# HGRN scores of a unit's two heads in one run of narrow matmuls, far and near parts in one PSUM bank

## The chip, the cores and the metric

The kernel runs on one core of a Trainium2 chip. A core has five engines with their own instruction queues, each of which works in order: TensorE (PE in the profile; its weight loads are listed apart as PEld), VectorE (DVE), ScalarE (ACT), GpSimd (POOL) and SyncE (SP), which issues most of the DMAs. Matmuls write to PSUM, an accumulator memory in banks; the other operands lie in SBUF. The metric is the device time of one execution in microseconds (us), the median of three.

## The reference

One layer of a hybrid decoder trunk on 256 tokens of width 2048. One input projection feeds three mixers of width 1024 (HGRN2, RG-LRU, Mamba-2 SSD) and their gates; each branch goes through its block of the output projection, is gated and added to the residual stream, and a final RMSNorm closes it.

```python
h = rmsnorm(x, norm_w[l])
proj = h @ w_in[l]
o_a = hgrn2_mixer(a_q, a_f, a_i, lower_bounds[l])
o_a = rmsnorm(o_a, hgrn_norm_w[l].reshape(A_HEADS, A_VAL)).reshape(bsz, s, BRANCH_WIDTH)
o_a = o_a * jax.nn.silu(a_z)
...
branch_out = jnp.einsum('bsnc,ncd->bsnd', branches, w_out[l].reshape(N_BRANCH, BRANCH_WIDTH, D_MODEL))
x = x + jnp.sum(gates * branch_out, axis=2).astype(x.dtype)
```

The change lies in `hgrn2_mixer`. It has 8 heads of 128 keys and 128 values. In each head the score of query t against key s is a sum over the keys of q·k times the product of the forget gates between s and t, and the output is the causal scores times the values.

## The kernel before, in words

**The weight stream.** All of the weights (140 tiles of 1 MB, `raw`) are read once by DMA. Each tile is cut into two halves. For each half ScalarE rounds it to `whi` (line 415) and VectorE forms the rest `wlo` (line 417); there are four buffers of each. TensorE uses a half in 12 matmuls of 512 columns (blocks by token: lines 523 to 525, three products for each of four pieces) or in 16 matmuls of 512 and 256 columns in turn (blocks by channel: lines 472 and 473). `whi` of a half can be written only when TensorE is through with the half four before it. These are called weight matmuls below.

**The mixers.** Everything else is written as Python generators ("streams"). A planner with a model clock for each engine (`Clock`, `Engine.cost`, `Streams.fits`) decides at build time between which weight matmuls a piece of a stream is put into the engines' queues. A stream gives way at each `yield`, whose letters name the engines that the next piece needs. The planner's cost of a matmul is four cycles per column, at least as many as for 128 rows or for the rows it loads; it does not know that narrow matmuls can run beside each other. Since the engines work in order, what the planner lays down is the order of execution.

**The HGRN stream.** `a_unit(i)` works on two heads, and there are four units, with their matmuls at about 469, 546, 613 and 689 us. For each head it makes 52 narrow matmuls, each with 32 rows of output, called a score run below: 4 of 128 columns (`px`, scores between the two halves of the sequence), 4 of 64 (`far64`), 4 of 32 (`far32`), and the near scores `pd`: 8 of 48 columns and 32 of 16. Then ScalarE copies `px` into the score tile `sc`, VectorE picks the near scores together in `dg` (one multiply with `id32`, five predicated copies) and copies `far64`, `far32` and `dg` into `sc`: together called the clearing of a head. Then two matmuls multiply `sc` with the values (`vt`): the value matmuls. `sc` has a tile for each of the two heads (`sc_3581` and `sc_3582` in the built program).

When both heads are done, ScalarE squares the output (`osq`), splits it into `two` (the upper part by ScalarE, the rest by VectorE), two matmuls sum the squares over a head (lines 1194 and 1195 before; called the norm matmuls), ScalarE makes the inverse root (three operations, `rq` last), VectorE applies it with the gate, and `split_branch` writes the result as `boh` (ScalarE) and `bol` (VectorE). These are the weights' partner in the output projection of branch 0. Its first block follows right behind the fourth unit: its first three halves of weights meet heads 0 to 5, the fourth half meets heads 6 and 7, which are the fourth unit's.

Before the change, the loop over the two heads holds everything from the score run to the value matmuls; each head takes two PSUM tiles, `pf` (far) and `pd` (near).

## Time and profile before

| | us |
|---|---|
| median of three runs | 830.51 (829.95 to 830.66) |
| the profiled execution | 830.41 |
| its span, from the first to the last instruction | 828.6 |
| PE busy in the span | 815.4 |
| DVE busy | 615.0 |
| ACT busy | 478.3 |

1.8 us of the execution lie outside the span. The span has some 10 us before the stream of weight matmuls starts and some 15 us behind the last one; between them PE is nearly always busy. In a timeline a row has the start in us, the time it covers, the engine, the line, the operation, output and inputs, the sizes and how many instructions of the kind are merged in it (x8), and, in brackets, how long the engine was idle before and what ended that. Line 161 is that of the helper through which all of the streams' operations go, so they are told apart by their tiles. A matmul of full 32-bit numbers, as in the score runs, is recorded twice.

### The profile page before, as it was taken

The numbers are of one execution on the slowest core, as the hardware profiler recorded it, in microseconds if no ns is written. First come the engines' busy times: TensorE is split into PE (matmuls) and PEld (weight loads), VectorE is DVE, ScalarE is ACT, GpSimd is POOL, SyncE is SP. The second block draws the span as 40 slices with busy tenths as digits, with TensorE's granted clock in tenths as the row PEclk, the third lists the DMA queues.
The fourth block names the chain that finished last, engine by engine and source line by source line (L and its number), as shares of the span: only waits on it lengthen the run. The fifth ranks groups of instructions, "written<-read, shape, count | busy, mean of one in ns | idle before, by whom it ended". The sixth has DMA issues, their size and how long they took to land.

```text
span 828.6 us, 12296 instructions
## 1 busy us (share of the span) xinstructions
PE 815.4 (98%) x4805; PEld 683.7 (83%) x4805; DVE 615.0 (74%) x976; ACT 478.3 (58%) x653; POOL 48.4 (6%) x103
## 2 busy tenths in 40 slices
PE   8999999999999999999999999999999999999995
PEld 8978887887888888888888888888888888888884
DVE  6578796987878787668786887688778868656463
ACT  6556455655665747645666556647655673754443
POOL 0000200020120000200100200000020000000000
PEclk9999999999999999999999999999999999999998
DMA  9947745565595555754465645553584455565522
GB/s 338 358 157 252 259 173 189 197 197 197 189 338 198 181 200 183 246 207 161 162 240 203 206 157 198 203 196 117 200 248 157 159 204 198 187 220 202 203 102 102
DMA packets 27401, 167.45 MB, mean 202 GB/s; under 512 B 3808, under 2 KB 4352, under 8 KB 9296
## 3 DMA queue, kind: packets, MB, share of 16 engines
q1 hardware_dynamic: 23360, 153.63, 52.7%
q0 software_dynamic: 3840, 12.96, 5.1%
q8 instruction: 37, 0.61, 0.3%
q10 hardware_dynamic: 144, 0.09, 0.1%
q14 instruction: 20, 0.16, 0.1%
HBM read 161.41 MB, written 5.26 MB: 201 GB/s over the span
## 4 chain that ended last, share of the span: by engine, by line
PE 95%; DVE 2%; ACT 1%; DMA 1%; issue 1%; SPq 0%; POOL 0%; POOLq 0%; DVEq 0%; ACTq 0%
PE ps L523 22%; PE ps L524 22%; PE ps L525 22%; PE ps L472 14%; PE ps L473 7%; PE pmt L161 3%; PE ps L485 2%; DMA raw<-w 1%; PE pmt L962 1%; ACT whi L415 0%; DVE wlo L417 0%; DVE sc L161 0%; ACT l L161 0%; PE ps L543 0%; PE ps L541 0%
## 5 line engine op out<-in xcount | busy, mean ns | idle before, releaser
L417 DVE TENSOR_TENSOR wlo<-raw,whi 128x1024 fp32r<-128x1024 f32 x275 | 332.7, 1221 | 165.7 <-ACT whi L415 165.0
L415 ACT CAST whi<-raw 128x1024 fp32r<-128x1024 f32 x275 | 286.8, 1051 | 286.8 <-PE ps L525 165.4
L523 PE MATMUL ps<-whi,hT 128*128 128x512 f32 x640 | 251.4, 393 | 0.0
L524 PE MATMUL ps<-wlo,hT 128*128 128x512 f32 x640 | 249.3, 390 | 0.0
L525 PE MATMUL ps<-whi,hT 128*128 128x512 f32 x640 | 249.3, 390 | 0.0
L472 PE MATMUL ps<-hT,whi 128*128 128x512 f32 x512 | 181.4, 397 | 0.0
L473 PE MATMUL ps<-hT,wlo 128*128 128x256 f32 x512 | 143.6, 280 | 0.0
L523 PEld LDWEIGHTS ps<-whi,hT 128*128 128x128 f32 x640 | 120.2, 188 | 25.7 <-issue 1.1
L525 PEld LDWEIGHTS ps<-whi,hT 128*128 128x128 f32 x640 | 120.1, 188 | 25.4
L524 PEld LDWEIGHTS ps<-wlo,hT 128*128 128x128 f32 x640 | 120.2, 188 | 24.0
L472 PEld LDWEIGHTS ps<-hT,whi 128*128 128x128 f32 x512 | 96.0, 188 | 23.1 <-issue 0.7
L473 PEld LDWEIGHTS ps<-hT,wlo 128*128 128x128 f32 x512 | 96.7, 189 | 0.5
L523 PE MATMUL ps<-whi,boh 128*128 128x512 f32 x176 | 69.2, 393 | 0.0
L524 PE MATMUL ps<-wlo,boh 128*128 128x512 f32 x176 | 68.6, 390 | 0.0
L525 PE MATMUL ps<-whi,bol 128*128 128x512 f32 x176 | 68.5, 389 | 0.0
L525 PEld LDWEIGHTS ps<-whi,bol 128*128 128x128 f32 x176 | 33.0, 188 | 6.9
L523 PEld LDWEIGHTS ps<-whi,boh 128*128 128x128 f32 x176 | 33.0, 188 | 6.7
L524 PEld LDWEIGHTS ps<-wlo,boh 128*128 128x128 f32 x176 | 33.1, 188 | 6.6
L134 ACT ACT_TABLE_LOAD x26 | 33.4, 1283 | 1.5 <-PEq L1474 1.2
L161 ACT ACTIVATE gt<-ps,rtok 128x512 f32<-128x512 f32 x36 | 23.7, 681 | 7.7 <-PE ps L525 6.9
L693 POOL DMA_DIRECT2D zd<-gt x12 | 6.6, 550 | 359.8 <-DVE gt L161 316.6
L707 POOL DMA_DIRECT2D gz<-zd x48 | 26.2, 552 | 15.0 <-DMA zd<-gt 14.4
(241 smaller groups left out, 669.4 us busy)
## 6 DMA issues: line engine op xcount, KB each, us to landing
raw<-w SPq DMA_DIRECT2D x137, 1024.0 KB, 4.8
zd<-gt POOLq DMA_DIRECT2D x12, 256.0 KB, 2.5
gz<-zd POOLq DMA_DIRECT2D x48, 64.0 KB, 5.1
raw<-w SPq DMA_DIRECT2D x5, 512.0 KB, 8.8
xsq<-xtok SPq DMA_DIRECT2D x2, 1024.0 KB, 10.6
brd<-sums POOLq DMA_DIRECT2D x4, 512.0 KB, 5.6
xacc<-xtok POOLq DMA_DIRECT2D x1, 2048.0 KB, 13.1
out_dram<-xacc SPq DMA_DIRECT2D x7, 256.0 KB, 2.4
```

Source lines behind the costliest of these rows:

```text
L134: self.eng.preload_act_table_set(self.set)
L161: return f(*a, **k)
L415: nc.scalar.copy(out=hi, in_=raw[:, sl])
L417: nc.vector.tensor_tensor(out=lo, in0=raw[:, sl], in1=hi.bitcast(F32), op=ALU.subtract)
L472: pe.matmul(ps[:, ct], lhsT=hi[:, c0:c0 + 128], rhs=flat(hT[:, k]), start=k == 0, stop=False)
L473: pe.matmul(ps[:, ct, S:], lhsT=lo[:, c0:c0 + 128], rhs=hT[:, k, 0], start=False, stop=k == KD - 1)
L485: pe.matmul(ps[:, ct], lhsT=(hi, lo)[i][:, c0:c0 + 128], rhs=hT[:, q * 4 + kk, j], start=q == 0 and n == 0, stop=q == 3 and n == last)
L523: pe.matmul(pss[j], lhsT=hi_ap(k, j), rhs=hi[:, sl], start=k == 0, stop=False)
L524: pe.matmul(pss[j], lhsT=hi_ap(k, j), rhs=lo[:, sl], start=False, stop=False)
L525: pe.matmul(pss[j], lhsT=lo_ap(k, j), rhs=hi[:, sl], start=False, stop=k == nk - 1)
L707: gp.dma_start(out=t[32 * q:32 * q + 32, 4 * j:4 * j + 4], in_=zd[q, :, j])
L962: pe.matmul(o, lhsT=wp[:, a, ct, g], rhs=xp[:, b, ct], start=u == 0, stop=u == 2)
```

## The change

The loop over the two heads is cut into three. The first makes both heads' score runs, one behind the other with no `yield` between them. Each head now has one PSUM tile: `pd` is a view of columns 224 to 447 of `pf`, behind `px`, `far64` and `far32`. The second loop clears the heads, with a `yield` between them. The third does the value matmuls of both.

```diff
         yield from st.get("pm", "p")
         op = pm.tile([P, 2, S], F32, name="pmt")
+        made = []
         for ct in range(2):
-            h = 2 * i + ct
             pf = pm.tile([P, 512], F32, name="pmt")
-            pd = pm.tile([P, 2, 112], F32, name="pmt")
+            pd = pf[:, 224:448].rearrange("p (j n) -> p j n", j=2)
             px, far64, far32 = pf[:, 0:128], pf[:, 128:192], pf[:, 192:224]
...
-            yield "va"
+            made.append((px, far64, far32, pd))
+        yield "va"
+        for ct, (px, far64, far32, pd) in enumerate(made):
             sc = A["sc"][ct]
             scd = sc[:, 0:3:2]
             dg = a2.tile([P, 2, 32], F32, name="dg")
...
             for u in range(0, P, 32):
                 dve.tensor_copy(out=scd[u:u + 32, :, u:u + 32], in_=dg[u:u + 32])
-            yield "p"
+            if ct == 0:
+                yield "va"
+        yield "p"
+        for ct in range(2):
+            h, sc = 2 * i + ct, A["sc"][ct]
             hv = slice(h * P, h * P + P)
             mm.matmul(op[:, ct], lhsT=vt[:, 0, hv], rhs=flat(sc[:, 0:2]), start=True, stop=False)
             mm.matmul(op[:, ct, P:S], lhsT=vt[:, 1, hv], rhs=sc[:, 2], start=False, stop=True)
```

No arithmetic is added or taken away. What moves is the order on each engine, since the planner now places other pieces. Up to the first unit's score runs (469 us) nothing moves. In all four units PE has 104 narrow matmuls in one run where it had 52 twice. Between that run and the first head's value matmuls stand 36 weight matmuls in the first and the fourth unit, 56 by channel in the second, and 15 by token and 28 by channel in the third; the second head's value matmuls follow 3 (by channel: 4) weight matmuls later. The third and fourth unit's runs come 30 weight matmuls later than before. Three places:

The first is on PE behind the fourth unit (`sc_3582` is the second head's score tile, `two` the input of the norm matmuls, `boh` and `bol` the output projection's). Before, the second head's value matmuls stand 24 weight matmuls ahead of the norm matmuls, whose surroundings are:

```order
L523 MATMUL ps<-whi,hT 128x512
L524 MATMUL ps<-wlo,hT 128x512
L525 MATMUL ps<-whi,hT 128x512
L1194 MATMUL pmt<-two,onesr 128x512
L1195 MATMUL pmt<-two,onesr 128x512
L523 MATMUL ps<-whi,hT 128x512
L524 MATMUL ps<-wlo,hT 128x512
L525 MATMUL ps<-whi,hT 128x512
L523 MATMUL ps<-whi,boh 128x512
```

With the change:

```order
L161 MATMUL pmt<-sc_3582,vt 128x256
L161 MATMUL pmt<-sc_3582,vt 128x128
L523 MATMUL ps<-whi,hT 128x512
L524 MATMUL ps<-wlo,hT 128x512
L525 MATMUL ps<-whi,hT 128x512
L1200 MATMUL pmt<-two,onesr 128x512
L1201 MATMUL pmt<-two,onesr 128x512
L523 MATMUL ps<-whi,boh 128x512
```

The norm matmuls stay where they were in the stream of weights, but for three matmuls; the value matmuls moved towards them, so that 3 weight matmuls are left between the two where there were 24.

The second is on ACT at the same place, from the squares of the fourth unit to its `boh` (`gt` is the gate of the output projection's first block):

```order
 L161 ACTIVATE osq<-pmt 128x512
 L161 CAST two<-osq 128x512
-L415 CAST whi<-raw 128x1024 x2
+L161 ACTIVATE gt<-ps,rtok 128x512 x2
 L134 ACT_TABLE_LOAD
 L161 ACTIVATE osq<-pmt,eps 128x512
 L161 ACTIVATE osq<-osq 128x512
 L161 ACTIVATE rq<-osq 128x512
-L134 ACT_TABLE_LOAD
-L161 ACTIVATE gt<-ps,rtok 128x512 x2
 L161 CAST boh<-osq 128x512
```

The two gate operations and the one table load that is left now stand ahead of the inverse root, and two roundings of weights went ahead of the squares or behind `boh`; the next `whi` after `boh` is that of the fourth half of the output projection's first block.

The third is on DVE, where a head is cleared, with the waits in brackets (`dg` collects the near scores; `Activation` is ScalarE's counter). It reads the same in all eight heads:

```order
 L161 TENSOR_TENSOR dg<-pmt,cs 128x64 [waits PE_49]
-L161 COPY_PREDICATED dg<-mk,pmt 128x32 [waits DVE_49]
+L161 COPY_PREDICATED dg<-mk,pmt 128x32 [waits Activation_49]
 L161 COPY_PREDICATED dg<-mk,pmt 128x2x16 [waits DVE_49]
 L161 COPY_PREDICATED dg<-mk,pmt 128x4x8 [waits DVE_49]
 L161 COPY_PREDICATED dg<-mk,pmt 128x8x4 [waits DVE_49]
 L161 COPY_PREDICATED dg<-mk,pmt 128x16x2 [waits DVE_49]
-L161 COPY sc_3581<-pmt 64x64 [waits Activation_49]
+L161 COPY sc_3581<-pmt 64x64 [waits Pool_49]
```

Before, ScalarE's copy of `px` waited for PE alone, and VectorE waited for it where it starts on `far64`. Now the copy waits for VectorE's first operation on the bank, and VectorE's second waits for the copy.

## The prediction

> **What bounds the kernel now.** I read the shares of the engines and the chain of waits first, then the waits between engines by tile, then the timelines of PE, DVE and ACT around the four units. The page's busy line, and from its fourth part the chain by engine:

> ```profile
> span 828.6 us, 12296 instructions
> PE 815.4 (98%) x4805; PEld 683.7 (83%) x4805; DVE 615.0 (74%) x976; ACT 478.3 (58%) x653; POOL 48.4 (6%) x103
> PE 95%; DVE 2%; ACT 1%; DMA 1%; issue 1%; SPq 0%; POOL 0%; POOLq 0%; DVEq 0%; ACTq 0%
> ```

> PE is busy for 815.4 of 828.6 us and makes 95% of the chain that sets the end. So time is won or lost only where PE's own work gets shorter or longer, or where PE stands still. It does stand still in this part of the kernel, but little. The list of waits, for PE on the scores (idle us, times, longest):

> ```profile
> PE pmt L161 <- DVE sc L161: 0.9, 2, 0.7
> ```

> The narrow matmuls, by their tile (count, then least, median and longest ns of one). They are told by pitch, not by these durations, since narrow matmuls lie over one another: 179 ns each times 104 would be 19 us a head.

> ```profile
> L161 PE MATMUL pmt<-ql,kl x640: 179/183/219, 469.6 to 698.3; 128*32 128x16 f32 x128, 128*32 128x64 f32 x16, 128*32 128x32 f32 x16
> ```

> **One run instead of two.** PE in the first unit: the last weight matmuls ahead, the start of the score run, its last group, and two weight matmuls behind.

> ```profile
> 468.84 0.39 PE L524 MATMUL ps<-wlo,hT 128*128 128x512 f32 x1
> 469.07 0.39 PE L525 MATMUL ps<-whi,hT 128*128 128x512 f32 x1
> 469.39 0.43 PE L161 MATMUL pmt<-ql,kx 128*32 128x128 f32 x8
> ...
> 470.27 0.45 PE L161 MATMUL pmt<-ql,kl 128*32 128x16 f32 x31
> 470.65 0.50 PE L523 MATMUL ps<-whi,hT 128*128 128x512 f32 x1
> 470.99 0.40 PE L524 MATMUL ps<-wlo,hT 128*128 128x512 f32 x1
> ```

> Starts are what counts. Two weight matmuls lie 0.23 us apart (468.84 and 469.07). The narrow run starts 0.32 behind the last of them, 0.09 more. At its end the last narrow matmul starts at 470.27 + 0.45 − 0.18 (one lasts 0.18) = 470.54, and the next weight matmul at 470.65: some 0.10 more than the step inside the run. The weight matmul after that comes 0.34 later and not 0.23: another 0.11. So a changeover into narrow matmuls and out of them takes 0.09 + 0.10 + 0.11 = 0.30. The run itself is 470.54 − 469.39 = 1.15 a head. The change makes no matmul fewer; it takes away one changeover in each of four units: 4 × 0.30 = **−1.20**. Not shown before is a second head that follows straight behind the first. If its eight 128-column matmuls bring back part of the 0.09 the saving is 0.20 a unit; if a run's slow start (0.88 for the 128, 64 and 48 columns and first 16, 469.39 to 470.27) is partly filling up, it is 0.45. That makes 0.8 to 1.8; I take 1.20, since it is read from the edges themselves.

> **Waits on the scores that go.** PE in the second unit, at the value matmuls of the first and of the second head, and in the third unit at the second head's:

> ```profile
> 553.11 0.28 PE L473 MATMUL ps<-hT,wlo 128*128 128x256 f32 x1
> 553.22 0.81 PE L161 MATMUL pmt<-sc,vt 128*128 128x256 f32 x4
> 553.79 0.47 PE L472 MATMUL ps<-hT,whi 128*128 128x512 f32 x1
> ...
> 563.68 0.28 PE L473 MATMUL ps<-hT,wlo 128*128 128x256 f32 x1
> 564.70 0.89 PE L161 MATMUL pmt<-sc,vt 128*128 128x256 f32 x4 [0.74 <-DVE sc L161]
> 565.34 0.48 PE L472 MATMUL ps<-hT,whi 128*128 128x512 f32 x1
> ```
> ```profile
> 625.26 0.39 PE L525 MATMUL ps<-whi,bol 128*128 128x512 f32 x1
> 625.82 0.89 PE L161 MATMUL pmt<-sc,vt 128*128 128x256 f32 x4 [0.18 <-DVE sc L161]
> 626.47 0.48 PE L523 MATMUL ps<-whi,boh 128*128 128x512 f32 x1
> ```

> The first head's do not wait: 0.11 from the 256-column matmul ahead, 0.57 to the next. The second head's wait: 1.02 and 0.64, so 0.91 + 0.07 = 0.98 more. In the third unit 0.56 for 0.23 and 0.65 for 0.57: 0.33 + 0.08 = 0.41. Together **−1.39**, if they don't come back. Whether they do is decided by the clearing, on DVE and on ACT in the first unit:

> ```profile
> 470.77 0.22 DVE L161 TENSOR_TENSOR dg<-pmt,cs 128x64 f32<-128x64 f32 x1 [1.01 <-PE pmt L161]
> 471.03 1.18 DVE L161 COPY_PREDICATED dg<-mk,pmt 128x32 f32<-128x32 uint8 x5
> ...
> 474.07 1.23 DVE L417 TENSOR_TENSOR wlo<-raw,whi 128x1024 fp32r<-128x1024 f32 x1
> ```
> ```profile
> 470.11 0.27 ACT L161 COPY sc<-pmt 128x128 f32<-128x128 f32 x1 [1.60 <-PE pmt L161]
> ```

> A head's clearing is 470.77 to 474.07 = 3.30 on DVE. The bank that far and near parts now share adds a handover: DVE's second operation waits for ACT's copy, 0.26 (470.11's 0.27, less what overlaps), and two passes between engines of some 0.04 each: 0.34, so 3.64 a head. From the run's start, the first head is made at 1.15 + 0.18 = 1.33, cleared at 4.97; with one `wlo` (1.23) between, the second at 9.84. PE reaches its value matmuls in units 1 and 4 behind a run of 2.40, 36 weight matmuls of 0.23, the first head's 0.57 and three more weight matmuls with their changeover 0.77: 12.0. In unit 2, 56 matmuls by channel (0.23 and 0.11 in turn: 9.5) put it at 13.3; in unit 3, 15 and 28 of the two kinds (8.2) at 12.0. Were DVE in a `wlo` when the run ends, it is 11.1 instead of 9.84. So 1 to 2 us are left everywhere. The handover is hidden by that cover; if it is gone, all of it stands on PE (third rival). Bounds of this term: 1.39 down to 0.

> What the rows speak against is a price for the shared bank: in before ACT's copy at 470.11 ran while PE was still filling the other bank. [...]

> **The fourth unit's tail.** This is where a new wait comes in. PE in before around the second head's value matmuls, and much later the last weight matmul of the first three halves:

> ```profile
> 702.46 0.39 PE L525 MATMUL ps<-whi,hT 128*128 128x512 f32 x1
> 702.68 0.81 PE L161 MATMUL pmt<-sc,vt 128*128 128x256 f32 x4
> 703.25 0.47 PE L523 MATMUL ps<-whi,hT 128*128 128x512 f32 x1
> ...
> 704.02 0.40 PE L523 MATMUL ps<-whi,hT 128*128 128x512 f32 x1
> ...
> 713.79 0.39 PE L525 MATMUL ps<-whi,bol 128*128 128x512 f32 x1
> ```

> ACT there, from the squares to `boh`:

> ```profile
> 703.53 0.60 ACT L161 ACTIVATE osq<-pmt 128x512 f32<-128x512 f32 x1 [1.65 <-PE pmt L161]
> 704.16 0.62 ACT L161 CAST two<-osq 128x512 fp32r<-128x512 f32 x1
> ...
> 706.96 1.05 ACT L415 CAST whi<-raw 128x1024 fp32r<-128x1024 f32 x1 [1.23 <-PE ps L525]
> ...
> 709.51 0.69 ACT L161 ACTIVATE osq<-pmt,eps 128x512 f32<-128x512 f32 x1 [0.20 <-PE pmt L1195]
> ...
> 711.55 1.28 ACT L134 ACT_TABLE_LOAD   x1
> 712.84 1.27 ACT L161 ACTIVATE gt<-ps,rtok 128x512 f32<-128x512 f32 x2
> ...
> 714.47 0.62 ACT L161 CAST boh<-osq 128x512 fp32r<-128x512 f32 x1 [0.35 <-DVE osq L161]
> 714.99 2.95 ACT L415 CAST whi<-raw 128x1024 fp32r<-128x1024 f32 x3
> ```

> And DVE:

> ```profile
> 706.91 0.69 DVE L161 TENSOR_TENSOR two<-osq,two 128x512 fp32r<-128x512 f32 x1
> ...
> 711.56 0.69 DVE L161 SCALAR_TENSOR_TENSOR rq<-pmt,rq 128x512 f32<-128x512 f32 x1 [2.29 <-ACT rq L161]
> ...
> 713.74 0.69 DVE L161 TENSOR_TENSOR osq<-osq,gz 128x512 f32<-128x512 f32 x1
> ```

> Let X be the start of the second head's value matmuls (702.68 here). ACT's square starts at X + 0.85, its `two` runs from X + 1.48 to 2.10, DVE's `two` takes 0.69 more: X + 2.83. Before, 24 weight matmuls (5.5 us) covered that. Now three are left, so PE is at the norm matmuls at X + 1.34 (704.02 − 702.68), and would leave them at X + 1.79. The first can go at X + 2.12, the second at X + 2.87, the next weight matmul at X + 3.10: PE stands for **1.31**. Queued behind them on PE is the whole of the output projection's first block.

> What is late next is its fourth half. The chain from X: `gt` on ACT 2.10 + 1.27 = 3.37; table load 1.28, 4.65; the three operations of the inverse root 709.51 to 711.53, 2.02, 6.67; DVE from `rq` to the end of `osq`, 711.56 to 714.43, with the handoffs 2.90, 9.57; `boh` 0.04 later until `whi` begins, 714.47 to 714.99, so 10.13; `whi` 1.05, 11.18; its `wlo` 1.23 and 0.04, 12.45. A PE that had waited for nothing would need that `wlo` at the half's second matmul, 36 + 1 behind the norm matmuls: 704.02 to 713.79 are 43 matmuls in 9.77, 0.227 each, so 1.79 + 8.40 = 10.19. PE is late by 12.45 − 10.19 = **+2.26** in all, 1.31 of it at the norm matmuls and 0.95 at the fourth half. Bounds: 1.9 if the half's first matmuls go ahead and two handoffs overlap, 2.7 if DVE has a `wlo` in the way at `two` for part of its 1.23. I take 2.26, since every term has its row.

> **The sum:** −1.20 − 1.39 + 2.26 = −0.33, on the profiled execution's own 830.41 (1.81 of it outside the span): 830.08. The median of the runs shown, 830.51, is 0.10 above that execution, so 830.2. With the bounds: 829.2 (1.8, 1.39 and 1.9 give −1.3) to 831.0 (0.8, half of 1.39 and 2.1 give about +0.5).

> **The rivals.** A difference of 0.2%, 1.66 us (828.85 and 832.17), is about what a measurement of this kernel can tell from no change.

> First, the tail doesn't hold PE: the two savings alone, −2.59, 827.9. For it: the profile's other places show PE covering such chains without a wait (before, the norm matmuls start at their pitch), and a PE that comes to X late finds ACT and DVE free. Against it: nothing in the order lets the norm matmuls go before both `two`, and the wait of 1.31 is counted from X itself. Chance 0.16.

> Second, the joined run saves nothing, since the second head's start and the slow part of the run cost as much inside as at an edge: +1.20 on the forecast, 831.4. For it: 0.88 of a head's 1.15 lie ahead of its last 31 narrow matmuls, so wide and narrow ones aren't alike. Against it: the 0.30 is read at the weight matmuls, which are simply fewer neighbours of narrow ones. Chance 0.12.

> Third, slower: the shared bank's handover stands on PE's path, ahead of the value matmuls. Its price is 8 heads × 0.34 = 2.72, so 832.9, and more with the old waits back. It decides from the point where the second head is cleared more than those 1 to 2 us later than worked out, as when ACT's copy sits behind a `whi` of 1.05 and a second `wlo` of 1.23 slips in. For it: before, PE waited at exactly these matmuls (0.74 and 0.18). Against it: 36 weight matmuls cover now. Chance 0.14.

> **How the numbers follow.** The forecast has 0.58, of which 0.04 lie below 828.85. Faster: 0.16 + 0.04 = 0.20; same: 0.54 + 0.12 = 0.66; slower: 0.14. The range goes from 827.6, which takes in most of the first rival, to 832.0, which takes in the second; the third and the rest of the first are left out, about 0.19.

> **What would show it.** In the changed kernel's PE timeline: one stretch of 2.3 to 2.5 us of narrow matmuls in each unit, with one changeover; no idle time by DVE's `sc` ahead of value matmuls in units 2 and 3; ahead of the norm matmuls (lines 1200 and 1201) idle time of about 1.3 us by `two`, and about 1 us by `whi` or `wlo` some 36 weight matmuls later. On DVE, `dg`'s second operation waits some 0.3 for ACT's `sc`. It is wrong if PE goes through the norm matmuls without a stop, if the fourth half waits much more than 1 us, if waits by `sc` appear anywhere, or if a second head's score run begins with a gap.

## The result and the profile after

The changed kernel takes 838.09 us (median of six, 835.25 to 841.02) and the kernel before, on the same chip, 830.59: a ratio of 1.0091 (95% interval 1.008 to 1.0101), 0.9% slower and clear of the noise. 830.2 was forecast, with 832.0 as the range's upper end. The spread of 5.8 us is new too: before it is 0.7.

The page of the changed kernel, its span, engines and chain:

```profile
span 836.2 us, 12297 instructions
PE 816.5 (98%) x4805; PEld 685.1 (82%) x4805; DVE 614.6 (73%) x976; ACT 478.2 (57%) x653; POOL 48.5 (6%) x103
PE 94%; issue 1%; ACT 1%; DMA 1%; DVE 1%; SPq 0%; POOL 0%; POOLq 0%; DVEq 0%; ACTq 0%
```

The span is 7.6 us longer with the same number of matmuls and nearly the same busy time. "issue" is time in which the engine waited for nothing that the profile shows. The list of waits says whose (total, times, longest):

```profile
PE pmt L161 <- issue: 4.7, 2, 3.8
PE ps L472 <- issue: 1.5, 1, 1.5
```

Neither row is there before, and the waits of PE on DVE's `sc` are gone. PE's timeline shows where it stands: in the joined runs of unit 1 and unit 3, and just behind the run of unit 2.

```profile
470.97 0.26 PE L161 MATMUL pmt<-ql,kl 128*32 128x16 f32 x9
472.12 0.34 PE L161 MATMUL pmt<-ql,kl 128*32 128x16 f32 x19 [0.89 <-issue]
...
472.41 0.46 PE L161 MATMUL pmt<-ql,kl 128*32 128x16 f32 x31
472.80 0.50 PE L523 MATMUL ps<-whi,hT 128*128 128x512 f32 x1
473.14 0.40 PE L524 MATMUL ps<-wlo,hT 128*128 128x512 f32 x1
...
549.62 0.28 PE L473 MATMUL ps<-hT,wlo 128*128 128x256 f32 x1
551.35 0.40 PE L472 MATMUL ps<-hT,whi 128*128 128x512 f32 x1 [1.46 <-issue]
...
622.63 0.21 PE L161 MATMUL pmt<-ql,kl 128*32 128x16 f32 x3
626.63 0.43 PE L161 MATMUL pmt<-ql,kl 128*32 128x16 f32 x28 [3.79 <-issue]
...
627.80 0.53 PE L523 MATMUL ps<-whi,boh 128*128 128x512 f32 x1
628.12 0.63 PE L524 MATMUL ps<-wlo,boh 128*128 128x512 f32 x1
...
631.45 0.39 PE L523 MATMUL ps<-whi,boh 128*128 128x512 f32 x1
```

In units 1 and 3 the matmuls on either side of the gap are of the same kind, in the middle of the second head's near scores: nothing that they read comes from DVE or ACT at that moment. In starts, PE loses 1.05 us in unit 1 (from 471.05, where the last of the nine starts, to 472.12, less a step), 1.62 in unit 2 (1.73 − 0.11) and 3.96 in unit 3. Behind unit 3 the weight matmuls also become slow. By windows (busy time of the engines, then PE's granted clock):

```profile
624.51:627.92 3.41, 1.29 (x32) 1.12 (x32) 0.99 (x6) 0.00 (x0) 0.00 (x0) 1.00 0.21 79
627.92:631.33 3.41, 3.41 (x10) 2.65 (x9) 1.83 (x4) 1.31 (x2) 0.00 (x0) 0.50 0.00 0
```

For 3.41 us the clock is 0.50, and a weight matmul takes 0.43 us and not 0.23: 3.65 us from 627.80 to 631.45 for 9 steps that take 2.05 at full speed, 1.60 lost. Together 1.05 + 1.62 + 3.96 + 1.60 = 8.2 us, which is more than the whole difference. So the rest of the change gained a little, about as forecast, and an unforeseen cost went on top.

The tail of unit 4 in the changed kernel, for later use:

```profile
713.28 0.81 PE L161 MATMUL pmt<-sc,vt 128*128 128x256 f32 x4
...
715.43 0.49 PE L1200 MATMUL pmt<-two,onesr 128*128 128x512 f32 x1 [0.63 <-ACT two L161]
716.16 0.50 PE L1201 MATMUL pmt<-two,onesr 128*128 128x512 f32 x1 [0.23 <-DVE two L161]
716.50 0.40 PE L523 MATMUL ps<-whi,boh 128*128 128x512 f32 x1
...
724.68 0.39 PE L523 MATMUL ps<-whi,boh 128*128 128x512 f32 x1
725.70 0.50 PE L524 MATMUL ps<-wlo,boh 128*128 128x512 f32 x1 [0.64 <-DVE wlo L417]
```

### The profile page after: what moved, and what is told of

Read it like the earlier page. It is cut to its first block, busy times and chain, and to the rows that moved or that the text cites. A ratio compares the mean times of both kernels' runs of the same rounds, so it can differ in the third digit from the quotient of the medians.

```text
span 836.2 us, 12297 instructions
## 1 busy us (share of the span) xinstructions
PE 816.5 (98%) x4805; PEld 685.1 (82%) x4805; DVE 614.6 (73%) x976; ACT 478.2 (57%) x653; POOL 48.5 (6%) x103
## 4 chain that ended last, share of the span: by engine, by line
PE 94%; issue 1%; ACT 1%; DMA 1%; DVE 1%; SPq 0%; POOL 0%; POOLq 0%; DVEq 0%; ACTq 0%
PE ps L523 22%; PE ps L524 22%; PE ps L525 22%; PE ps L472 14%; PE ps L473 7%; PE pmt L161 3%; PE ps L485 2%; DMA xc_t<-xT 1%; PE pmt L962 1%; ACT whi L415 0%; ACT osq L161 0%; PE ps L543 0%; PE ps L542 0%; PE ps L541 0%; DVE xacc L161 0%
## 5 line engine op out<-in xcount | busy, mean ns | idle before, releaser
L417 DVE TENSOR_TENSOR wlo<-raw,whi 128x1024 fp32r<-128x1024 f32 x275 | 332.9, 1220 | 167.1 <-ACT whi L415 166.7
L415 ACT CAST whi<-raw 128x1024 fp32r<-128x1024 f32 x275 | 286.8, 1050 | 281.9 <-PE ps L525 161.0
L523 PE MATMUL ps<-whi,hT 128*128 128x512 f32 x640 | 251.3, 393 | 0.0
L525 PE MATMUL ps<-whi,hT 128*128 128x512 f32 x640 | 249.3, 389 | 0.0
L524 PE MATMUL ps<-wlo,hT 128*128 128x512 f32 x640 | 249.3, 389 | 0.0
L472 PE MATMUL ps<-hT,whi 128*128 128x512 f32 x512 | 181.6, 398 | 1.5 <-issue 1.5
L473 PE MATMUL ps<-hT,wlo 128*128 128x256 f32 x512 | 143.5, 280 | 0.0
L523 PEld LDWEIGHTS ps<-whi,hT 128*128 128x128 f32 x640 | 120.2, 188 | 25.5 <-issue 1.1
L525 PEld LDWEIGHTS ps<-whi,hT 128*128 128x128 f32 x640 | 120.1, 188 | 25.4
L524 PEld LDWEIGHTS ps<-wlo,hT 128*128 128x128 f32 x640 | 120.2, 188 | 24.0
L472 PEld LDWEIGHTS ps<-hT,whi 128*128 128x128 f32 x512 | 96.1, 188 | 23.1 <-issue 0.7
L473 PEld LDWEIGHTS ps<-hT,wlo 128*128 128x128 f32 x512 | 96.7, 189 | 2.0 <-issue 1.5
L524 PE MATMUL ps<-wlo,boh 128*128 128x512 f32 x176 | 69.4, 394 | 0.6 <-DVE wlo L417 0.6
L523 PE MATMUL ps<-whi,boh 128*128 128x512 f32 x176 | 69.4, 394 | 0.0
L525 PE MATMUL ps<-whi,bol 128*128 128x512 f32 x176 | 69.1, 393 | 0.0
L524 PEld LDWEIGHTS ps<-wlo,boh 128*128 128x128 f32 x176 | 33.3, 189 | 7.8 <-DVE wlo L417 1.1
L525 PEld LDWEIGHTS ps<-whi,bol 128*128 128x128 f32 x176 | 33.5, 190 | 7.1
L523 PEld LDWEIGHTS ps<-whi,boh 128*128 128x128 f32 x176 | 33.5, 190 | 6.9
L161 ACT ACTIVATE gt<-ps,rtok 128x512 f32<-128x512 f32 x36 | 23.9, 683 | 7.7 <-PE ps L525 6.9
## 6 DMA issues: line engine op xcount, KB each, us to landing
xsq<-xtok SPq DMA_DIRECT2D x2, 1024.0 KB, 11.1
```

The costliest lines, as they stand in the source:

```text
L161: return f(*a, **k)
L415: nc.scalar.copy(out=hi, in_=raw[:, sl])
L417: nc.vector.tensor_tensor(out=lo, in0=raw[:, sl], in1=hi.bitcast(F32), op=ALU.subtract)
L472: pe.matmul(ps[:, ct], lhsT=hi[:, c0:c0 + 128], rhs=flat(hT[:, k]), start=k == 0, stop=False)
L473: pe.matmul(ps[:, ct, S:], lhsT=lo[:, c0:c0 + 128], rhs=hT[:, k, 0], start=False, stop=k == KD - 1)
L523: pe.matmul(pss[j], lhsT=hi_ap(k, j), rhs=hi[:, sl], start=k == 0, stop=False)
```

## The theories

If PE waits for none of its operands, it may wait for its own instructions. The page has a queue that carries them (packets, MB, share; the same row before and after), the third queue of its third part:

```profile
q8 instruction: 37, 0.61, 0.3%
```

PE runs 4805 weight loads and 4805 matmuls. 0.61 MB over 37 packets is 16.4 KB a packet, and 37 packets for some 9,660 instructions make about 261 instructions a packet (an estimate). A full 32-bit matmul counts four instructions in the trace (two loads, two matmuls), so a head's score run is 208 instructions and a joined run 416. Counting PE's instructions in the trace from the first one, the three gaps stand ahead of numbers 5057, 6337 and 7361, which lie 1280 and 1024 apart. The largest number that goes into both distances is 256, near the 261: 256 instructions are called a **block** below. Each gap is then 193 above a multiple of 256, and they lie five and four blocks apart. Three gaps with one remainder are the ground for the first theory.

**Instruction supply**: a block is asked for when PE's queue enters the block before it, and arrives some microseconds later. This is a theory, worked out from the packets' times in the trace of the changed kernel: each of the 37 starts between 43 instructions before and 256 behind a place that is 193 above a multiple of 256, and they take one such place after another. The one that starts 256 behind, at 624.21, is that ahead of unit 3's gap: PE had come to number 7361 and went on 1.44 us after it had ended. A weight matmul is two instructions in 0.23 us, so a block of them lasts 29 us, and in the kernel before PE has no wait by "issue". A joined run does 256 instructions in 1.4 us (1.15 us for 208). It then catches up with the next block, if the first block's end lies so early in the run that the second one's lies in it too, or just behind it.

Rivals: the **shared bank** (the handover, or two engines at one bank, holds PE up), and the **join as such** (two heads' operands, or any run of narrow matmuls that is this long).

## The experiments

**One shift, nothing else.** Eight narrow matmuls more at the start of the program, where PE waits for its first weights; everything behind keeps its order and moves by 32 in the count.

```diff
     for _ in range(WARM):
         pe.matmul(warm, lhsT=ones, rhs=ones, start=True, stop=True)
+    for _ in range(8):
+        pe.matmul(warm[0:32, 0:16], lhsT=ones[:, 0:32], rhs=ones[:, 0:16], start=True, stop=True)
```

> Instruction-supply theory: the changed kernel's three stalls by 'issue' all stand at the same place in PE's instruction stream counted in blocks of 256 (instructions 5057, 6337 and 7361, each 193 above a multiple of 256), since the next block comes only some 3.7 us (unit 3: 5.5 us) after PE's sequencer enters the one before, and a joined run of 416 instructions goes through a block in 1.4 us. Eight narrow matmuls (32 instructions) more at the very start of the program, with no other edit, move the stalls by 32 instructions back in each run: unit 1's goes away (its run then begins some 4 us after the request), unit 2's comes into the run, 26 instructions before its end, about 1 to 4 us long, unit 3's stands at the 331st instruction of its run and not at the 363rd, unit 4 has none. The time is within 835 to 840 us. Shared-bank or operand theory: 32 instructions at the start change nothing; the stalls stand at the same matmuls of units 1 and 3 (the 293rd and 363rd instruction), with the same 838 us.

It took 837.2 us (ratio 1.0077, interval 1.0063 to 1.0092). PE's timeline of this kernel in unit 2 and unit 3:

```profile
547.97 0.32 PE L161 MATMUL pmt<-ql,kl 128*32 128x16 f32 x17
550.38 0.31 PE L161 MATMUL pmt<-ql,kl 128*32 128x16 f32 x14 [2.09 <-issue]
550.62 0.50 PE L474 MATMUL ps<-hT,whi 128*128 128x512 f32 x1
...
625.89 0.21 PE L161 MATMUL pmt<-ql,kl 128*32 128x16 f32 x2 [1.79 <-issue]
```

Unit 1 has no gap. Unit 2's has moved from behind the run into it, with 14 matmul records left: with their loads, the 26 instructions of the expectation but for one record. Unit 3's stands at the 331st instruction. The numbers are again 6337 and 7361: the gaps stayed where they were in the count, and the matmuls moved past them. No theory in which a particular matmul waits allows for that.

**The bank undone, the join kept.**

```diff
         made = []
+        pfs = pm.tile([P, 2, 224], F32, name="pmt")
+        pds = pm.tile([P, 2, 2, 112], F32, name="pmt")
         for ct in range(2):
-            pf = pm.tile([P, 512], F32, name="pmt")
-            pd = pf[:, 224:448].rearrange("p (j n) -> p j n", j=2)
+            pf, pd = pfs[:, ct], pds[:, ct]
```

> One part undone: both heads' runs stay joined and the order on every engine stays, but far parts (of both heads) and near parts (of both heads) lie in different PSUM banks again, so ScalarE's copy and VectorE's near part no longer share one. Instruction-supply theory: PE's instructions and their count are the same, so the stalls stay at instructions 5057, 6337 and 7361 and the time stays at 835 to 841 us. Shared-bank theory: the stalls go, 830 us. On DVE the 0.4 us wait of dg for sc goes in either case.

839.54 us (1.011, 1.0093 to 1.0127). The gaps stand at 5057, 6337 and 7361 as before the edit:

```profile
474.30 0.34 PE L161 MATMUL pmt<-ql,kl 128*32 128x16 f32 x19 [3.13 <-issue]
```

Unit 1 now loses 3.3 us where it lost 1.05, with the same instructions: a gap's place is fixed, its length is not. So the shared bank isn't the cause.

**The bank alone.** The kernel before, with one line of the change: `pd` is a view of `pf`.

> The other part alone: the kernel before with each head's near scores moved into the bank of its far scores, runs not joined; PE's order is that of before. Instruction-supply theory: no run is over 208 instructions, so no stall by 'issue'; the handover costs 0.34 us a head on DVE, which lands on PE only at the second heads of units 2 and 3, where PE waited already: 830.6 + 0.7 = 831.3 us at most. Shared-bank theory: 836 us or more, with idle time in or behind the score runs.

831.04 us (1.0008, 0.9999 to 1.0016), no gap by "issue". What it costs stands at the second heads of units 2 and 3 (before: 0.74 and 0.18):

```profile
564.62 0.89 PE L161 MATMUL pmt<-sc,vt 128*128 128x256 f32 x4 [0.89 <-DVE sc L161]
626.03 0.89 PE L161 MATMUL pmt<-sc,vt 128*128 128x256 f32 x4 [0.57 <-DVE sc L161]
```

0.15 and 0.39 more. On DVE the handover costs more than the forecast's 0.34 a head, since at one head DVE waits 3.3 us for ACT's copy (total, times, longest):

```profile
DVE dg L161 <- ACT sc L161: 5.8, 8, 3.3
```

But it lands on PE only where PE was waiting for a head's clearing already, and nowhere else; its measured effect on the time, 0.7 us, is at the edge of what can be told.

**All ends of blocks put right, join and bank kept.** 25 narrow matmuls more at the start, and 30 and 48 weight matmuls written as two of half the width, so that a block ends either in the middle of a run (instructions 192 and 202 of units 1 and 3), with the next end behind it, or at its very start (6 and 8 in units 2 and 4). At the very start, if PE's queue runs some 40 instructions ahead of execution (an estimate from the packets' times), it enters the block while weight matmuls of 0.23 us are still being done.

```diff
+    def mm512(h, o, lhsT, rhs, start, stop):
+        if TWO.get(h, 0):
+            TWO[h] -= 1
+            for c in (0, 256):
+                pe.matmul(o[:, c:c + 256], lhsT=lhsT, rhs=rhs[:, c:c + 256], start=start, stop=stop)
...
-                    pe.matmul(pss[j], lhsT=hi_ap(k, j), rhs=hi[:, sl], start=k == 0, stop=False)
+                    mm512(h0 + q, pss[j], lhsT=hi_ap(k, j), rhs=hi[:, sl], start=k == 0, stop=False)
```

> The changed kernel with its joined runs and its shared banks, and with PE's instruction stream shifted so that no run holds the end of a block at a bad place: 25 narrow matmuls (100 instructions) more at the start of the program, 30 of the 512-column weight matmuls between units 1 and 2 and 48 between units 3 and 4 written as two of 256 columns. Instruction-supply theory: no stall by 'issue' in units 1 to 4 and no reduced clock after unit 3, so what is left is the forecast's sum: 829.6 to 830.6 us, with the 1.4 and 0.9 us waits of unit 4's tail. If joined runs stall for another reason: 836 to 841 us as with the change.

832.22 us (1.0025, 1.0015 to 1.0036): 6 us of the 7.5 are back, and in the profiled execution the mean granted clock is 0.996, as in the kernel before (0.994 in the changed kernel), but it is 2 us more than expected, and the expectation of no stall was missed. Two parts of that are in the trace. Two block ends, 33 and 42 instructions behind the runs of units 1 and 3 (numbers 5313 and 7617, the same remainder), still hold PE up, by 0.30 and 0.67 us:

```profile
474.80 0.39 PE L521 MATMUL ps<-whi,boh 128*128 128x512 f32 x1
475.33 0.50 PE L521 MATMUL ps<-wlo,boh 128*128 128x512 f32 x1
...
625.12 0.40 PE L474 MATMUL ps<-hT,whi 128*128 128x512 f32 x1
626.03 0.29 PE L475 MATMUL ps<-hT,wlo 128*128 128x256 f32 x1 [0.50 <-issue]
```

The first is not the block's alone. Its matmul needs a `wlo` that DVE finished at 475.16, and the list of waits puts it down to that. Where PE waits for `wlo` in unit 4's tail, it goes on 0.05 us behind it; so 0.18 of the 0.30 would have been lost anyway.

And a matmul in two halves isn't free: a half takes 0.120 us from start to start and a whole one 0.227, 13 ns more for each of the 78, 1.0 us in all. With these the forecast's 830.1 becomes 832.1. That is near the median, but the figures are of the profiled execution, which took 831.50. In it unit 1's run, ahead of which only cheap matmuls were added, starts 0.48 us earlier than in the kernel before (468.91 for 469.39); less this, the sum is 831.6. The nine executions go from 831.2 to 835.7, so gaps may well come back in some of them.

**Nothing of the change but the length.** The kernel before, a head at a time and in two banks, with each head's 52 score matmuls issued a second time through the plain engine (the planner counts nothing for them, so its order stays).

> The kernel before, with nothing of the change in it (a head at a time, far and near parts in two banks, PE's order of before), but each head's 52 score matmuls are issued twice, the second time over the first: eight runs of 416 instructions. Instruction-supply theory: counted in blocks of 256, the ends of blocks fall at instruction 36, 81, 6, 20, 105, 149, 102 and 134 of the eight runs and again 256 later, so six of them (36, 81, 105, 149, 102, 134) and perhaps the one at 20 stall by 'issue' at the second one, 1 to 4 us each and 1.7 us more where the clock then halves; all stalls at the same remainder, 193, as with the change. 830.4 + 8 x 1.15 for the doubled work + 8 to 25 = 848 to 865 us. If it is the two heads together, the shared bank or the changed order that stalls PE: 839.6 us and no time by 'issue'.

861.83 us (1.0376, 1.036 to 1.0391). Exactly the six runs named stall, at numbers 5057, 5569, 8129, 8641, 9665 and 10177, all 193 above a multiple of 256; the runs with a block's end at their 6th and 20th instruction do not. The list of waits (two source lines, since some of the doubled matmuls stand at each):

```profile
PE pmt L1179 <- issue: 13.6, 5, 4.5
PE pmt L1176 <- issue: 3.6, 1, 3.6
```

So a run of 416 instructions in one go is enough, with one head, two banks and the old order, if a block ends at a bad place in it.

The packets of q8 in the traces say the same. At each of the gaps at this remainder named so far, 16 in five kernels, PE goes on 1.24 to 1.48 us after the end of the last packet before it, whatever the gap's length and whichever matmul comes next.

**The waits' term by itself.** The kernel before, with the second head's value matmuls of units 2 and 3 held back by a few weight matmuls.

```diff
+            n0 = spents[0] + {(1, 1): 8, (2, 1): 6}.get((i, ct), 0)
+            while spents[0] < n0:
+                yield ""
             yield "p"
             hv = slice(h * P, h * P + P)
```

> The kernel before, with one thing of the change by another way: the second head's value matmuls of units 2 and 3 are held back by four (by channel) and three weight matmuls, so that PE does 0.69 and 0.68 us of work in the time it waited for DVE's sc; runs apart, two banks, all other matmuls where they stood. The forecast's term for the waits: 0.69 of the 0.98 us in unit 2 and the 0.41 in unit 3 are saved, 830.4 - 1.1 = 829.3 us (829.0 to 829.7), and 'sc' waits of at most 0.3 us are left. If the gain of that term was never there to be had: 830.2 to 830.6.

829.17 us (0.9986, 0.9977 to 0.9994), as expected. What is left of unit 2's wait is 0.2 us in starts (0.31 for 0.11):

```profile
564.19 0.28 PE L476 MATMUL ps<-hT,wlo 128*128 128x256 f32 x1
564.50 0.89 PE L161 MATMUL pmt<-sc,vt 128*128 128x256 f32 x4
```

This trace also holds a small gap that the list of waits doesn't name for PE. It lies in the second run of unit 3, which has only 208 instructions. Its last 31 matmuls of 16 columns, in the kernel before and here:

```profile
620.85 0.45 PE L161 MATMUL pmt<-ql,kl 128*32 128x16 f32 x31
```
```profile
619.92 0.69 PE L161 MATMUL pmt<-ql,kl 128*32 128x16 f32 x31
```

0.25 us are lost ahead of number 7361, the same remainder, 1.34 us after the end of a packet that came, with the queue put some 40 instructions ahead of execution (the estimate above), 4.6 us after PE's queue had entered the block before. Before, the packet for the same place ended 1.79 us ahead of it: just early enough.

**A version that is faster than both.** The same, with only unit 1 joined and a block's end put at the 232nd instruction of its run by 15 narrow matmuls at the start of the program.

> The same with unit 1's two runs joined as in the change (its two heads in shared banks; units 2 to 4 as before), and 15 narrow matmuls (60 instructions) more at the start of the program, which put the end of a block at instruction 232 of the joined run and the next 72 instructions behind it. Instruction-supply theory: no stall by 'issue' at this run, and the join's 0.3 us is earned: 829.0 us (828.6 to 829.4). If joined runs stall wherever they stand: 830.3 or more.

828.56 us (0.9978, 0.9969 to 0.9987), 1.8 us below the kernel before; PE has no gap by "issue" in any unit. The step from 829.17 to 828.56 is twice the join's 0.30 for one unit, and within the spread of the two; the small gap, which is not there in this version's trace, may be the rest of it.

## Why the prediction was wrong

**The join, −1.20.** Right in mechanism and size. In unit 1, from the last weight matmul ahead (469.03) to the second behind (473.14), less the gap's 1.05 and two steps of 0.23, a joined run costs 2.60; before, two runs cost 2 × (1.92 − 0.46) = 2.92. That is 0.32 for a forecast 0.30 (unit 4, whose run has no gap, gives 0.37). The second rival, that the second head starts like a new run, falls with it.

**The waits, −1.39.** Right. No `sc` wait is left on PE in the changed kernel, and the same waits, filled in another way, were worth 1.2 us.

**The bank.** Right that a head's chain grows by about 0.34: from the list of waits of the changed kernel,

```profile
DVE dg L161 <- ACT sc L161: 2.8, 8, 0.4
```

or 0.35 a head, and 36 or more weight matmuls cover it. The third rival, the handover on PE's path, didn't come about in the changed kernel. It is real in the order of before, at the two places named for it.

**The tail of unit 4, +2.26.** Right. The first weight matmul behind the norm matmuls starts 3.22 us after the second head's value matmuls (716.50 − 713.28), for 3.10 forecast and 1.79 without a wait: 1.43 for 1.31. At the fourth half two steps take 1.36 us (724.68 to 726.04) for 0.46: 0.90 for 0.95. Together 2.33. So the first rival, a tail that doesn't hold PE, falls too.

**What failed** is the step "One run instead of two", where it takes a head's 1.15 us as a length that can be laid end to end, with bounds of 0.8 to 1.8 us of gain. That price held only as long as PE's instructions were at hand. It had been read from runs of 208 instructions, each with slow weight matmuls on both sides, and 208 is less than a block: in the trace of before PE nowhere used up a block faster than the next one came, though in one place it was close, as the small gap with the waits' term shows. The changed kernel goes beyond what any row of before showed. Neither the bounds nor a rival held a loss from the run's own length, and so no case reached 838. (The forecast's upper case, 0.8, half of 1.39 and 2.1, comes to +0.6 and not +0.5, and leaves out the tail's own upper bound of 2.7; neither changes that.) The part on what would prove the forecast wrong asked only about a gap where the second head begins; the gap stands well inside it.

**The sum again:** −1.28 − 1.39 + 2.33 + 8.2 = +7.9, for a measured 7.6 in the span; some 0.3 us stay unexplained.

**What stays open** is what sets the length of a gap. From the point where PE's queue enters a block (put some 40 instructions ahead of execution, an estimate: the earliest packet starts 41 before a place that is 193 above a multiple of 256) to the next block's packet, the 37 blocks of before took 2.0 us in the mean where the DMA engines had been over 80% busy in the microsecond ahead (15 of them), and 0.7 where under 20% (16); then 1.0 us for the packet, and in units 1 to 3 of the changed kernel 1.4 to 1.5 more until PE went on. That fits packets that wait behind the weight loads, which would explain the 5.8 us between executions, but it is not shown: in unit 3 the DMA engines' busy share was 0.00 in the first half microsecond after PE's queue had entered the block (at some 621.1) and 0.51 in the second, and the packet still came only at 624.2; and no run was made with other traffic.

## What to carry to other kernels

A price read from a run of small instructions may hold for its length only, as here that of 1.15 us for 208 instructions: before joining runs, count instructions as well as time, and look whether the stretch uses up instructions faster than any stretch of the profile did. Where an engine stands still by "issue", number its instructions: gaps with the same remainder at 256, as the 193 here, point to their supply, and the test is whether the code moves past them with a few cheap instructions at the start of the program. Where several runs stand at different remainders, one shift may not mend all of them (32 instructions took away unit 1's gap alone); keep such a run well under a block, with slow instructions on both sides (208 with slow neighbours lost at most 0.25 us here), or join only those whose place allows it.

## What the runs showed of the hardware

```profile
623.26:626.68 3.42, 1.63 (x117) 1.50 (x108) 2.69 (x15) 0.27 (x1) 0.00 (x0) 1.00 0.88 302
626.68:630.09 3.41, 3.41 (x9) 2.64 (x9) 1.38 (x3) 1.04 (x1) 0.00 (x0) 0.50 0.04 14
```
```profile
624.98:628.39 3.41, 1.65 (x162) 1.55 (x149) 0.00 (x0) 0.27 (x1) 0.00 (x0) 1.00 0.71 233
628.39:631.81 3.42, 3.16 (x40) 2.67 (x40) 2.42 (x13) 1.23 (x2) 0.00 (x0) 1.00 0.21 84
```

By these windows a stall of 2 us could cost up to 1.7 us more (half of 3.41, an estimate; 1.60 was lost in the changed kernel).
